# Gate and up projections of a two-layer decoder trunk: 18 of 22 blocks by Strassen's seven products

## The chip, the cores and the metric

One core of one Trainium2 chip runs the whole program. The metric is the device time of one execution in microseconds (us), lower is better. The kernel before took 1387.57 us, the median of three runs (1387.44 to 1389.32).

## What is computed

Two layers, each a token mixer (a gated linear recurrence and sparse attention side by side, not touched here) and a feed-forward block, each followed by a layer norm of `ALPHA * x + sublayer(x)`. All tensors are float32: x has 512 tokens of 1024 values, the hidden width D_FF is 2816.

```python
def layer_norm(x, g, b, eps=1e-5):
    mu = jnp.mean(x, -1, keepdims=True)
    var = jnp.mean(jnp.square(x - mu), -1, keepdims=True)
    return (x - mu) * lax.rsqrt(var + eps) * g + b

for l in range(DEPTH):                                   # DEPTH = 2
    mix = token_mixer(x, l) @ w_out[l]
    x = layer_norm(ALPHA * x + mix, ln1_g[l], ln1_b[l])
    ffn = (jax.nn.silu(x @ w_ffn_gate[l]) * (x @ w_ffn_up[l])) @ w_ffn_down[l]
    x = layer_norm(ALPHA * x + ffn, ln2_g[l], ln2_b[l])
```

The change concerns `x @ w_ffn_gate` and `x @ w_ffn_up`, and what comes right behind them.

## The kernel before

**Precision.** Float32 operands go to TensorE as two parts, a rounded high part and the remainder (type fp32r). `mm3` (lines 77 to 82) makes one product of three matmuls: high x high (L79), high x low (L80), low x high (L81). In the trace, xh and xl are the parts of x, whi and wlo those of a weight.

**Weights.** `load_w` (L53 to L75) loads 512 KB of raw weight by SP's DMA queue into one of two buffers (wraw, L57), casts it on ScalarE to the high part (L73) and subtracts on VectorE for the low part (L74). There are three buffers each for whi and wlo. A helper tag `"a"` splits into one of eleven large buffers instead, where the weight can be kept.

**Gate and up.** The 2816 hidden columns are 22 blocks of 128. For each block there is one product for gate and one for up: `feat_mm` runs 8 steps over the 1024 inputs, each with `mm3` on all 512 tokens, so 24 matmuls of 512 columns. The weight stands still in the array, the tokens stream, and the result is 128 hidden columns x 512 tokens in a PSUM bank (tag "d", two banks). `feats` runs the blocks one after the other; only the first five products (`LEAD2`) go by halves of 256 tokens, since x arrives by halves from `norm_turn` (the norm ahead of the stage, which turns the rows by TensorE transposes and splits them). `ffn` takes each result: Silu on ScalarE for gate (L845), and for up the product on VectorE (L851) and the split of the hidden block into its two parts (L852, L853), which stay in SBUF.

**Down.** `wide_mm` takes hidden blocks as the stationary operand and streams 512 columns of the down weight. The first pass does the left 512 output columns of all four token tiles; then come tiles 0 and 1, and tiles 2 and 3, for the right ones. The last three weights of one pass are kept for the next. In the last layer four more weights (`held`, tag "a") are kept for the very end, where tile 2 runs its last matmuls ahead of tile 3, so that the output norm of tile 2 (`norm`, L617 on) lies beside the matmuls of tile 3.

**The order.** A scheduler (the Tile framework) orders the instructions of each engine by its own simulation and by priorities; `tc.high_priority(offset=...)` moves an instruction ahead. SP's queue carries the weight loads. POOL (GpSimd) issues the DMAs of its own queue (bias strips, residual rows, norm parameters) and computes the powers of the norms (L354, L614). The buffers of the mixer (bias strips and the like) are used again by tag when they are free. The lines that carry most of the stage:

```python
def feat_mm(self, pt, w, x, n0=0, n1=S, k0=0, k1=NK):                       # L85
    for k in range(k0, k1):
        self.mm3(pt[:, n0:n1], *w(k * 128, 128), XH[k // 4][:, k % 4, n0:n1],
                 XL[k // 4][:, k % 4, n0:n1], k == 0, k == NK - 1)
srcs = [s for u in range(NF) for s in (io["wg"][l, u], io["wu"][l, u])]
self.feats(srcs[:5], x1, ffn, LEAD2)
self.norm_rest(l, 0, rows, None)
self.feats(srcs[5:], x1, lambda i, pt: ffn(i + 5, pt))
held = (0, 1, 2, 3) if last else (0,)
late = list(held) if last else []
```

## Time and profile before

| | |
|---|---|
| median of three runs | 1387.57 us (1387.44 to 1389.32) |
| the profiled execution, its own time | 1386.79 us |
| its span in the profile | 1385.0 us |
| TensorE (PE) busy | 97% of the span |
| VectorE (DVE) busy | 54% |
| ScalarE (ACT) busy | 43% |
| GpSimd (POOL) busy | 8% |
| mean granted TensorE clock | 0.996 of full speed |

The profile is of one execution; its time is the span and 1.8 us around it. PE rows are matmuls, PEld rows are the loads of the stationary operand, which run beside them. Matmuls overlap one another, so the duration of one row is longer than the distance from its start to the next one's: the distance is what the stream costs.

### The profile page before, as it was taken

Reading aid. Unit: us, or ns where it says so; the run is one execution under the profiler, and the core shown is the slowest. Engines: PE = TensorE matmul, PEld = TensorE weight load, DVE = VectorE, ACT = ScalarE, POOL = GpSimd, SP = SyncE. Lnnn points to the kernel's source line nnn. Section 1 sums busy time; section 2 is a strip of 40 time slices with the busy share of each in tenths; the row PEclk is TensorE's granted clock in tenths of the full one; section 3 lists DMA queues with packets and bytes.
Section 4 is the critical chain, followed back from the end, with each engine's and each line's share of the span. In section 5 each row is a group of like instructions: output and inputs, shape, how many; then the busy total and the mean of one; then the engine's idle time right before and its main releaser. Section 6 shows DMA issues by size and latency. Waiting matters only on the chain.

```text
span 1385.0 us, 19299 instructions
## 1 busy us (share of the span) xinstructions
PE 1349.5 (97%) x7548; PEld 1172.0 (85%) x7548; DVE 754.4 (54%) x1483; ACT 594.1 (43%) x1109; POOL 106.8 (8%) x179
## 2 busy tenths in 40 slices
PE   7999999999999999999999999999999999999997
PEld 6978999789888888888889889987998888888885
DVE  4755898865633333224468568988636333332344
ACT  4244777844332232222443558777353232232220
POOL 2230111100000000000112001110000000000001
PEclk9999999999999999999999999999999999999999
DMA  6253213132222322234543222120413322322332
GB/s 225 87 148 113 77 56 105 42 118 88 73 96 91 106 91 94 104 104 140 182 135 113 77 84 77 61 100 32 137 47 122 106 92 93 106 91 96 132 107 92
DMA packets 39371, 139.84 MB, mean 101 GB/s; under 512 B 5188, under 2 KB 5348, under 8 KB 38768
## 3 DMA queue, kind: packets, MB, share of 16 engines
q1 hardware_dynamic: 31392, 112.93, 24.1%
q0 software_dynamic: 6736, 23.58, 5.3%
q10 hardware_dynamic: 1152, 2.10, 0.5%
q8 instruction: 59, 0.97, 0.3%
q14 instruction: 32, 0.26, 0.1%
HBM read 134.34 MB, written 7.10 MB: 102 GB/s over the span
## 4 chain that ended last, share of the span: by engine, by line
PE 88%; DMA 4%; ACT 3%; DVE 2%; issue 1%; POOL 0%; POOLq 0%; DVEq 0%; SPq 0%; ACTq 0%
PE ps_d L79 20%; PE ps_d L80 20%; PE ps_d L81 19%; PE ps_s L81 3%; PE ps_s L80 3%; PE ps_s L79 3%; PE ps_t L547 2%; PE ps_t L80 1%; PE ps_t L81 1%; PE ps_t L79 1%; PE ps_h L292 1%; PE ps_o L558 1%; PE ps_o L81 1%; PE ps_o L80 1%; PE ps_o L79 1%
## 5 line engine op out<-in xcount | busy, mean ns | idle before, releaser
L73 ACT CAST whi<-wraw 128x1024 fp32r<-128x1024 f32 (+1 forms) x190 | 199.3, 1049 | 534.3 <-PE ps_d L80 201.6
L74 DVE TENSOR_TENSOR wlo<-wraw,whi 128x1024 fp32r<-128x1024 f32 (+1 forms) x190 | 232.2, 1222 | 305.8 <-ACT whi L73 300.5
L79 PE MATMUL ps_d<-xh,whi 128*128 128x512 f32 (+1 forms) x888 | 338.2, 382 | 1.9 <-ACT gates L398 1.8
L81 PE MATMUL ps_d<-xh,wlo 128*128 128x512 f32 (+1 forms) x888 | 338.4, 381 | 0.0
L80 PE MATMUL ps_d<-xl,whi 128*128 128x512 f32 (+1 forms) x888 | 338.3, 381 | 0.0
L79 PEld LDWEIGHTS ps_d<-xh,whi 128*128 128x128 f32 x888 | 166.9, 188 | 33.0 <-ACT gates L398 1.9
L80 PEld LDWEIGHTS ps_d<-xl,whi 128*128 128x128 f32 x888 | 167.2, 188 | 31.9 <-issue 0.7
L81 PEld LDWEIGHTS ps_d<-xh,wlo 128*128 128x128 f32 x888 | 167.1, 188 | 31.2
L851 DVE TENSOR_TENSOR silu<-ps_d,silu 128x512 f32<-128x512 f32 x42 | 29.0, 691 | 130.0 <-PE ps_d L81 128.6
L79 PE MATMUL ps_d<-whi,xh 128*128 128x256 f32 (+1 forms) x304 | 90.8, 300 | 0.0
L80 PE MATMUL ps_d<-wlo,xh 128*128 128x256 f32 (+1 forms) x304 | 89.1, 294 | 0.0
L81 PE MATMUL ps_d<-whi,xl 128*128 128x256 f32 (+1 forms) x304 | 88.2, 291 | 0.0
L508 ACT ACTIVATE e<-e,mn 128x128 f32<-128x128 f32 (+3 forms) x128 | 71.6, 561 | 13.8 <-DVE mn L506 13.1
L614 POOL TENSOR_TENSOR rstd<-mv,mhalf 128x1 f32<-128x1 f32 x16 | 17.7, 1109 | 735.2 <-DVE mv L612 735.2
L506 DVE CUSTOM_DVE_ANT_0 e<-ps_s,strip 128x128 f32<-128x128 f32 (+3 forms) x128 | 59.2, 484 | 6.8 <-PE ps_s L521 5.9
L80 PEld LDWEIGHTS ps_d<-wlo,xh 128*128 128x128 f32 x304 | 58.3, 192 | 2.1 <-issue 1.4
L552 DVE TENSOR_TENSOR ptl<-ps_t,pth 128x384 fp32r<-128x384 f32 (+1 forms) x96 | 56.8, 595 | 5.5 <-ACT pth L551 4.7
L79 PEld LDWEIGHTS ps_d<-whi,xh 128*128 128x128 f32 x304 | 58.1, 192 | 1.8 <-issue 0.7
L551 ACT CAST pth<-ps_t 128x384 fp32r<-128x384 f32 (+1 forms) x96 | 48.7, 510 | 24.9 <-PE ps_t L547 17.4
L81 PEld LDWEIGHTS ps_d<-whi,xl 128*128 128x128 f32 x304 | 58.1, 191 | 0.7
L547 PE MATMUL ps_t<-ident,e 128*128 128x128 f32 x320 | 53.4, 273 | 0.3 <-ACT e L532 0.2
L324 DVE TENSOR_TENSOR hgKQ<-hgKQ,hgF 128x512 f32<-128x512 f32 x64 | 43.7, 686 | 6.0 <-PE ps_h L292 2.9
(475 smaller groups left out, 2590.0 us busy)
## 6 DMA issues: line engine op xcount, KB each, us to landing
wraw<-in_wd SPq DMA_DIRECT2D x55, 512.0 KB, 3.3
wraw<-in_wg SPq DMA_DIRECT2D x44, 512.0 KB, 3.2
wraw<-in_wu SPq DMA_DIRECT2D x44, 512.0 KB, 3.3
wraw<-in_wf SPq DMA_DIRECT2D x32, 512.0 KB, 3.6
wraw<-in_wt SPq DMA_DIRECT2D x16, 512.0 KB, 3.5
wraw<-in_wo SPq DMA_DIRECT2D x16, 512.0 KB, 3.2
w<-in_w POOLq DMA_DIRECT2D x16, 256.0 KB, 5.0
strip<-Z POOLq DMA_DIRECT2D x16, 256.0 KB, 3.0
```

The lines of the kernel that those rows point to most:

```text
L73: nc.scalar.copy(h, raw[:, i:i + n])
L74: nc.vector.tensor_tensor(o, raw[:, i:i + n], h.bitcast(F32), op=OP.subtract)
L79: first = t.matmul(out, ah, bh, start=start, stop=False)
L80: t.matmul(out, ah, bl, start=False, stop=False)
L81: t.matmul(out, al, bh, start=False, stop=stop)
L324: nc.vector.tensor_tensor(both, both, f, op=OP.mult)
L506: nc.vector.tensor_tensor_reduce(out=e, in0=pa, in1=st[:, 512 - pa.shape[-1]:], scale=1.0, scalar=3e38, op0=OP.add, op1=OP.min, accum_out=mn)
L508: nc.scalar.activation(e, e, AF.Exp, bias=mn, scale=-1.0, accum_out=sm)
L547: nc.tensor.transpose(p[:, c:c + 128], E[qt][:, j * 128:(j + 1) * 128], self.ident)
L551: nc.scalar.copy(ph[:, :c], p[:, :c])
L552: nc.vector.tensor_tensor(pl[:, :c], p[:, :c], ph[:, :c].bitcast(F32), op=OP.subtract)
L851: nc.vector.tensor_tensor(s, pt, s, op=OP.mult)
```

## The change

18 of the 22 blocks (4 to 21) of gate and of up are taken two by two. For such a pair, a unit, the weight is a matrix of 2 x 2 quarters (two blocks of 128 hidden columns x two halves of 512 inputs), and x one of 2 x 2 quarters (two halves of inputs, `R1.` and `R2.`, x two halves of 256 tokens, `R.1` and `R.2`). The four quarters of the result come from seven products of quarters (Strassen's scheme in Winograd's form) where eight are needed otherwise. A product has 4 steps x 3 matmuls of 256 columns, 12 matmuls. There are 9 pairs x 2 weights x 2 layers = 36 units.

- **Sums of x** (T1 to T4) are formed and split once per layer on VectorE and ScalarE, from the raw x1 that `norm_turn` now writes into buffers that stay.
- **Sums of weights**, four per unit. s1 and s3 come from a plain load on SP's queue and a second DMA on POOL's queue that adds to what is there (`accum_op`). The other two are formed on VectorE in the buffer of the raw weight.
- **Splits.** Each of the seven left operands is split on its own, 512 columns at a time (L111 on ScalarE, L112 on VectorE), into a ring of six places that is cut from the three whi and wlo buffers.
- **Sums of products.** A, D and B are accumulators of 256 columns in banks "d", "t", "s". Four products go into A and two into D, with a copy (sx, sy, su) taken by ScalarE in between; VectorE adds the copies to get the quarters. The last two products of a unit are placed among the next unit's.
- **Hidden blocks.** Blocks 0 to 5 are split at once; the other 16 stay whole in float32 and are split beside the first down pass into the large buffers, four at first and then two per step.
- **The end of the last layer.** The large buffers are taken, so nothing is held from the pass of tiles 0 and 1; the four late weights (now blocks 4 to 7 of the down weight's steps) are loaded again.

```diff
+    def stage(self, sa, sb):
+        with self.tc.high_priority(offset=3000):
+            a = self.sb.tile([128, 1024], F32, name="wraw", tag="wr", bufs=2)
+            s1, s3, d = (self.sb.tile([128, 512], F32, name=n, tag=t, bufs=2) for n, t in (("ws1", "st"), ("ws3", "pc"), ("wd", "wd")))
+            nc.sync.dma_start(s1, sb[:, 512:])
+            nc.sync.dma_start(s3, sa[:, :512])
+            nc.gpsimd.dma_start(s1, sb[:, :512], accum_op=OP.add)
+            nc.gpsimd.dma_start(s3, sb[:, :512], accum_op=OP.add)
+            nc.sync.dma_start(a, sa)
+            nc.sync.dma_start(d, sb[:, 512:])
+        return a, s1, s3, d
+
+    def split(self, raw):
+        h, o = self.ring[self.place % 6]
+        self.place += 1
+        with self.tc.high_priority(offset=3000):
+            nc.scalar.copy(h, raw)
+            nc.vector.tensor_tensor(o, raw, h.bitcast(F32), op=OP.subtract)
+        return h, o
+
+    def prod(self, acc, raw, R, start):
+        L = self.split(raw)
+        for k in range(4):
+            self.mm3(acc, *(p[:, k * 128:(k + 1) * 128] for p in L), *(p[:, k] for p in R), start and k == 0, k == 3,
+                     skip_group_check=not start)
+
+    def seven(self, units, R):
...
+        for unit in units + [None]:
+            if unit:
+                a, s1, s3, d = self.stage(*unit[:2])
+                A, B, D = (self.ps(t)[:, :256] for t in "dst")
+                self.prod(A, a[:, :512], R["R11"], True)
+                x = copy("sx", A)
+            if old:
+                old[0]()
+            if unit:
+                self.prod(D, s1, R["T1"], True)
+                y = copy("sy", D)
+                with self.tc.high_priority(offset=3000):
+                    nc.vector.tensor_tensor(a[:, :512], s1, a[:, :512], op=OP.add)
+                self.prod(B, a[:, 512:], R["R21"], True)
+                unit[2]("11", B, x)
+            if old:
+                old[1]()
+            if unit:
+                self.prod(A, a[:, :512], R["T2"], False)
+                u = copy("su", A)
+                with self.tc.high_priority(offset=3000):
+                    nc.vector.tensor_tensor(a[:, 512:], a[:, :512], a[:, 512:], op=OP.add)
+                self.prod(D, a[:, 512:], R["R22"], False)
+                unit[2]("12", D, u)
+                def third(A=A, s3=s3, y=y, take=unit[2]):
+                    self.prod(A, s3, R["T3"], False)
+                    take("22", A, y)
+                def fourth(A=A, d=d, take=unit[2]):
+                    self.prod(A, d, R["T4"], False)
+                    take("21", A, None)
+                old = (third, fourth)
...
-        srcs = [s for u in range(NF) for s in (io["wg"][l, u], io["wu"][l, u])]
+        srcs = [io[w][l, j] for j in range(4) for w in ("wg", "wu")]
...
+        self.seven([(io[w][l, j], io[w][l, j + 1], f(j)) for j in range(4, NF, 2) for w, f in (("wg", gate), ("wu", up))], R)
...
-        held = (0, 1, 2, 3) if last else (0,)
+        held = () if last else (0,)
...
-        late = list(held) if last else []
+        late = (4, 5, 6, 7) if last else ()
...
+        for i in late:
+            kept[i] = down_w(1, i, "a")
```

The takers `gate` and `up` (new lines 989 to 1014) add a copy to an accumulator's quarter on VectorE where the scheme wants it (L1009 for up), and then apply Silu on ScalarE (gate) or the product of gate and up on VectorE (up, L1011).

**VectorE, in the middle of gate and up of layer 0, before.** wlo is the split of a weight, silu the product of up and gate, h_f a split of a hidden block; per block (two weights) there are four instructions.

```order
L74 TENSOR_TENSOR wlo_4519<-wraw_4516,whi_4518 128x1024
L853 TENSOR_TENSOR h_f_3613<-silu_4413,h_f_3613 128x512
L74 TENSOR_TENSOR wlo_4552<-wraw_4549,whi_4551 128x1024
L851 TENSOR_TENSOR silu_4480<-ps_d_4488,silu_4480 128x512
L74 TENSOR_TENSOR wlo_4586<-wraw_4583,whi_4585 128x1024
```

**The same place of the change.** Here ws1 and ws3 are the sums by DMA, wraw and wd raw weights, sx and su copies of accumulators, up_5494 the up quarters that are being added together.

```order
L112 TENSOR_TENSOR wlo_4047<-wraw_5544,whi_4046 128x512
L112 TENSOR_TENSOR wlo_4047<-ws3_5420,whi_4046 128x512
L147 TENSOR_TENSOR wraw_5544<-ws1_5545,wraw_5544 128x512
L1009 TENSOR_TENSOR up_5494<-ps_s_5429,sx_5445 128x256
L112 TENSOR_TENSOR wlo_4043<-ws1_5545,whi_4042 128x512
L112 TENSOR_TENSOR wlo_4043<-wraw_5544,whi_4042 128x512
L156 TENSOR_TENSOR wraw_5544<-wraw_5544 128x512
L112 TENSOR_TENSOR wlo_4045<-wd_5421,whi_4044 128x512
L1009 TENSOR_TENSOR up_5494<-ps_t_5430,su_5525 128x256
L112 TENSOR_TENSOR wlo_4045<-wraw_5544,whi_4044 128x512
L1011 TENSOR_TENSOR h_e_5367<-up_5494,h_e_5367 128x512
L112 TENSOR_TENSOR wlo_4043<-ws3_5546,whi_4042 128x512
```

Splits are now half as long and stand between sums of weights (L147, L156) and additions from PSUM (L1009); a gate and an up unit together have 27 instructions on VectorE, 25 of them between the split of one ws1 buffer and the addition L147 that reads the next contents of the same buffer. On PE, the products of two units alternate so that 24 to 28 matmuls stand between two additions to the same accumulator with a copy or an addition between them.

**SP's queue, at the end of layer 0's mixer, before:** the last two output weights (in_wo), then the first of gate and up.

```order
L57 DMA wraw_3256<-in_wo 128x1024
L57 DMA wraw_3262<-in_wo 128x1024
L57 DMA wraw_3637<-in_wg 128x1024
L57 DMA wraw_3644<-in_wu 128x1024
L57 DMA wraw_3651<-in_wg 128x1024
```

**The same place of the change:**

```order
L97 DMA ws1_4049<-in_wg 128x512
L97 DMA ws1_4145<-in_wu 128x512
L57 DMA wraw_3256<-in_wo 128x1024
L98 DMA ws3_4050<-in_wg 128x512
L98 DMA ws3_4146<-in_wu 128x512
L57 DMA wraw_3262<-in_wo 128x1024
L57 DMA wraw_3628<-in_wg 128x1024
```

The plain halves of the sums for the first two units are loaded ahead of the third and fourth output weight; their buffers are those of bias strips. On POOL, the two adding DMAs of ws1 stand between the four powers of the mixer's last part (L354 before, L440 now), the second of them right ahead of the last power.

**VectorE at the end of the program, before.** r are the rows of a token tile, ps_o and ps_h the accumulators of tiles 2 and 3 in the last pass.

```order
L874 SCALAR_TENSOR_TENSOR r<-r,ps_o 128x512
L875 BN_STATS st<-r 128x6
L611 BN_AGGR mv<-st 128x2
L612 TENSOR_SCALAR mv<-mv 128x1
L621 SCALAR_TENSOR_TENSOR r<-r,mv,lnp 128x1024
L624 SCALAR_TENSOR_TENSOR r<-r,rstd,lnp 128x1024
L874 SCALAR_TENSOR_TENSOR r<-r,ps_h 128x512
L875 BN_STATS st<-r 128x6
L611 BN_AGGR mv<-st 128x2
```

**The same place of the change:**

```order
L1050 SCALAR_TENSOR_TENSOR r<-r,ps_o 128x512
L1051 BN_STATS st<-r 128x6
L1050 SCALAR_TENSOR_TENSOR r<-r,ps_h 128x512
L697 BN_AGGR mv<-st 128x2
L1051 BN_STATS st<-r 128x6
L698 TENSOR_SCALAR mv<-mv 128x1
L707 SCALAR_TENSOR_TENSOR r<-r,mv,lnp 128x1024
L697 BN_AGGR mv<-st 128x2
L710 SCALAR_TENSOR_TENSOR r<-r,rstd,lnp 128x1024
```

The two tiles' chains now alternate: on PE the matmuls of tiles 2 and 3 are interleaved, and ps_o ends 5 matmuls ahead of ps_h, where it ended 24 ahead before.

## Rows read from the trace of the kernel before

**Rows 1.** The page, busy time of each engine and share of the span.

```profile
PE 1349.5 (97%) x7548; PEld 1172.0 (85%) x7548; DVE 754.4 (54%) x1483; ACT 594.1 (43%) x1109; POOL 106.8 (8%) x179
```

**Rows 2.** By stretch: length, busy (count) PE PEld DVE ACT POOL, clock, DMA share, GB/s.

```profile
329.00:358.00 29.00, 29.00 (x244) 28.84 (x245) 9.32 (x18) 16.87 (x27) 1.96 (x3) 1.00 0.21 74
358.00:564.60 206.60, 206.60 (x922) 171.42 (x921) 80.42 (x86) 59.52 (x76) 0.00 (x0) 1.00 0.28 95
564.60:625.00 60.40, 60.40 (x267) 49.86 (x266) 15.91 (x14) 13.57 (x14) 0.00 (x0) 1.00 0.31 105
```

**Rows 3.** PE's timeline (start, duration, instruction): 512-column matmuls, first and last of 13.

```profile
361.64 0.39 PE L80 MATMUL ps_d<-xl,whi 128*128 128x512 f32 x1
...
364.36 0.39 PE L80 MATMUL ps_d<-xl,whi 128*128 128x512 f32 x1
```

**Rows 4.** PE's timeline in the lead blocks: 256-column matmuls, first and last of 17.

```profile
340.73 0.28 PE L81 MATMUL ps_d<-xh,wlo 128*128 128x256 f32 x1
...
342.64 0.28 PE L81 MATMUL ps_s<-xh,wx 128*128 128x256 f32 x1
```

**Rows 5.** Groups, 329 to 343 us, weight loads: count, busy, mean ns, idle before.

```profile
L81 PEld LDWEIGHTS ps_s<-xh,wx 128*128 128x128 f32 x14 | 2.6, 188 | 0.0
```

**Rows 6.** Groups by form, whole span, VectorE.

```profile
L74 DVE TENSOR_TENSOR wlo<-wraw,whi 128x1024 fp32r<-128x1024 f32 x186 | 228.1, 1226 | 300.0 <-ACT whi L73 294.7
...
L74 DVE TENSOR_TENSOR wx<-wraw,wx 128x512 fp32r<-128x512 f32 x24 | 16.3, 687 | 4.8 <-ACT wx L73 3.8 <-PE ps_o L566 0.9
...
L397 DVE TENSOR_TENSOR vt<-ps_d,vt 128x256 fp32r<-128x256 f32 x8 | 3.2, 417 | 0.0
```

**Rows 7.** Groups by form, whole span, ScalarE.

```profile
L845 ACT ACTIVATE silu<-ps_d 128x512 f32<-128x512 f32 x40 | 23.4, 585 | 0.0
...
L73 ACT CAST wx<-wraw 128x512 fp32r<-128x512 f32 x24 | 14.1, 618 | 18.1 <-DMA wraw<-in_wg 7.4 <-DMA wraw<-in_wu 3.7 <-DMA wraw<-in_wo 3.0
...
L295 ACT COPY atm<-ps_h 128x256 f32<-128x256 f32 x6 | 2.2, 365 | 9.5 <-PE ps_h L292 9.5
```

**Rows 8.** DMA issues: count, size of each, median us from issue to landing.

```profile
wraw<-in_wg SPq DMA_DIRECT2D x44, 512.0 KB, 3.2
...
strip<-Z POOLq DMA_DIRECT2D x16, 256.0 KB, 3.0
...
Z<-rv POOLq DMA_DIRECT2D x8, 320.0 KB, 9.8
```

**Rows 9.** DMA queues, POOL's: packets, MB, share of 16 engines.

```profile
q0 software_dynamic: 6736, 23.58, 5.3%
```

**Rows 10.** VectorE's timeline at the end, in brackets the idle time before.

```profile
1370.26 0.69 DVE L874 SCALAR_TENSOR_TENSOR r<-r,ps_o 128x512 f32<-128x512 f32 x1 [9.17 <-PE ps_o L81]
...
1373.73 1.28 DVE L624 SCALAR_TENSOR_TENSOR r<-r,rstd,lnp 128x1024 f32<-128x1024 f32 x1 [0.44 <-POOL rstd L614]
1375.70 0.69 DVE L874 SCALAR_TENSOR_TENSOR r<-r,ps_h 128x512 f32<-128x512 f32 x1 [0.68 <-PE ps_h L81]
...
1379.17 1.41 DVE L624 SCALAR_TENSOR_TENSOR r<-r,rstd,lnp 128x512 f32<-128x512 f32 x2 [0.44 <-POOL rstd L614]
```

**Rows 11.** PE's timeline: first and last L79 of the last pass, layers 0 and 1.

```profile
663.78 0.39 PE L79 MATMUL ps_o<-whi,h_qs 128*128 128x512 f32 x1
...
693.69 0.39 PE L79 MATMUL ps_h<-whi,h_qs 128*128 128x512 f32 x1
...
1346.86 0.39 PE L79 MATMUL ps_o<-whi,h_qs 128*128 128x512 f32 x1
...
1374.82 0.39 PE L79 MATMUL ps_h<-wa,hb 128*128 128x512 f32 x1
```

**Rows 12.** Timelines at the end of layer 0's mixer: VectorE, SP's queue, POOL.

```profile
273.98 0.69 DVE L506 CUSTOM_DVE_ANT_0 e<-ps_s,strip 128x512 f32<-128x512 f32 x1
...
277.90 0.33 SPq L57 DMA_DIRECT2D wraw<-in_wo  x1
...
279.00 1.04 POOL L354 TENSOR_TENSOR rs<-ss,mhalf 128x4 f32<-128x4 f32 x1 [3.43 <-DVE ss L352]
```

More of the change, by code (lines that the diff above doesn't have):

```diff
@@ new lines, in seven, with copy @@
+    def seven(self, units, R):
+        nc = self.nc
+        ts = [[self.sb.tile([128, 1024], F32R, name=n, tag=t, bufs=3) for n, t in (("whi", "wh"), ("wlo", "wl"))] for _ in range(3)]
+        self.ring = [[t[:, c:c + 512] for t in p] for p in ts for c in (0, 512)]
+        self.place = 0
+        def copy(name, src):
+            t = self.sb.tile([128, 256], F32, name=name, tag="a7", bufs=6)
+            with self.tc.high_priority(offset=4000):
+                nc.scalar.copy(t, src)
+            return t
+        old = None
+        for unit in units + [None]:
[29 more added lines that the diff above has]
+                old = (third, fourth)
@@ new lines, in gate, with take @@
+        def gate(j):
+            def take(part, acc, add):
+                if part == "11":
+                    raws[j], raws[j + 1] = hidden(j), hidden(j + 1)
+                g = raws[j + int(part[0]) - 1]
+                o = g[:, 256 * int(part[1]) - 256:256 * int(part[1])]
+                with tc.high_priority(offset=4000):
+                    if add is not None:
+                        nc.vector.tensor_tensor(o, acc, add, op=OP.add)
+                    if part == "12":
+                        nc.scalar.activation(g, g, AF.Silu)
+                    elif part[0] == "2":
+                        nc.scalar.activation(o, o if add is not None else acc, AF.Silu, scale=-1.0)
+            return take
```

118 lines of the change are left out of this document (91 added, 27 removed).

## The prediction

> **What bounds the kernel now.** I read the page's busy shares first: TensorE (PE) works 97% of the span, VectorE 54%, ScalarE 43% [rows 1]. Then the table by stretch, for the stage that is rewritten: from 358 us to 564.6 us, gate and up of layer 0, PE is busy all the time, with VectorE at 80 of 206.6 us, ScalarE at 60 and the DMA engines at 28% [rows 2]. A busy PE can still be slow, so the third view is PE's timeline. The 512-column matmuls of this stage each last 0.39 us there, but start every 0.227 us: the two rows are the first and the last of 13, 2.72 us apart [rows 3]. They overlap, nothing else is between them, and the stage lasts as many spacings as it has matmuls. So only PE's spacing and its number of matmuls count here, and everything else is free until it makes PE wait.
>
> **The change, part by part.**
>
> *Fewer, shorter matmuls.* A unit (one weight, two blocks) was 2 blocks x 8 x 3 = 48 matmuls of 512 columns, 48 x 0.2267 = 10.88 us. It is now 7 products x 4 x 3 = 84 of 256 columns. What one of these costs when the weights stand still and x streams can be read in the lead blocks of the same stage, which go by halves of the tokens: 17 rows, first and last 1.91 us apart, 16 spacings of 0.1194 us [rows 4]. So 84 x 0.1194 = 10.03 us. There are 9 pairs x 2 weights x 2 layers = 36 units: 36 x 0.85 = **-30.6 us**. The loss by half columns is thus small: two such matmuls take 0.239 us against 0.227 us. What speaks against it is the weight load, which is now twice as frequent for the same columns. Its rows read 0.188 us each in the same stretch [rows 5], longer than the 0.1194 us between matmuls, so successive loads must overlap one another or the matmuls. If they did not, they alone would take 84 x 0.188 = 15.8 us a unit, 36 x 4.9 = 177 us more than before; rows 4 exclude that for this very form. The Trainium skill (TensorE: Matmul & The Clock Gate, The mechanism) says that a weight load overlaps matmuls in flight only where it goes to another row group; by it the full-height loads here would lie between the matmuls and the change would lose. The rows of this case disagree with it.
>
> *VectorE and ScalarE in a unit.* VectorE now does 7 splits and 2 sums of 512 (0.687 us each), 3 additions of 256 from PSUM (0.417) and, for up, one product of 512 and two of 256 [rows 6]: 7.4 us for gate, 9.0 us for up, 8.2 of 10.03 us on the mean. ScalarE does 7 casts of 512 (0.618) and 3 copies of 256 from PSUM (0.365), and for gate a Silu of 512 and two of 256 (0.585 bounds the one, 0.365 the others) [rows 7]: 5.4 to 6.7 us. Neither reaches PE. What may cost is not the sum but a late hand-over: before PE may add to an accumulator again, a copy or an addition must have read it, and the order leaves 24 to 28 matmuls, 2.9 us or more, in between. Two splits already at work (1.4 us) and the addition itself (0.4) fit. No row shows such a chain at this load; I bound it by nothing and by 0.28 us a unit (one split's tail in every third unit or so), **0 to +10 us, taken +3**, since the spare ring places let the splits run several products ahead.
>
> *Loads.* A unit fetches 1792 KB where it fetched 1024: 183 GB/s over 10.03 us. Packets of the POOL queue moved 23.58 MB in 5.3% of 16 engines' span [rows 9], 321 GB/s when all work, so 5.7 us of each 10.03, or 7.3 if an adding DMA moves its bytes twice. The cover is the double buffers. The tile of s1 is free again after its split in one unit and its successor is wanted 25 VectorE instructions later, of 27 in two units: 18 us. In these lie the plain load (a load of twice its size lands in 3.2 us) and the adding DMA. Of the latter no row exists: its near end is the plain 256 KB transfer on POOL's queue, 3.0 us, its far end the slowest of that queue, 9.8 us for 320 KB [rows 8]. Even 3.2 + 9.8 fits into 18, so I cost it **nothing**; the nearer row in size and kind is the 3.0.  The raw weights have some 9 us for 3.2. The other cost would be throughput; that is a rival below.
>
> *The four sums of x.* 4 sums and 4 splits of 1024 on VectorE, at 1.23 us [rows 6] 9.8 us, and 4 casts on ScalarE, about 1 us each. They lie beside the lead blocks, where VectorE works 9.3 of 29 us [rows 2], and three plain blocks: **0**, and if that cover were gone, the first unit would wait some microseconds, twice.
>
> *Staged loads ahead of others.* The first two units' s1 tiles reuse the bias strips' buffers, so their loads stand on SP's queue ahead of the third output weight, and their adding DMAs stand on POOL's queue ahead of the last head's power. The last strip is read until 274.67 us; the output weight was issued at 277.90, the power at 279.00 [rows 12]. A load issued at 274.7 lands at about 277.9: **0**, with 1.1 us to spare; late, it would delay the end of the mixer by as much as it is late.
>
> *Splits of the hidden blocks.* 16 blocks x 2 halves are split beside the first down pass: 32 x 0.417 = 13.3 us of VectorE in 60 us, which has 15.9 busy [rows 2]. **0.**
>
> *The end.* The four weights of the last pass are no longer kept but loaded again, and the order now lets both last token tiles end together. The third tile's chain, 1370.26 to 1375.01, lay under the fourth's 24 matmuls; now only 5 matmuls (1.1 us) cover it [rows 10]. Of its 4.75 us, 0.44 were a wait that now gets filled, 1.1 stay covered: up to +3.2; with the fourth's own wait filled too, +1.9. **Taken +2.5.** The pass with these loads has its model in layer 0, where it loaded seven: from the first to the last of its rows 29.91 us, against 27.96 us in layer 1 with four kept [rows 11]. Next-layer loads disturb that one too: **0 to +2, taken +1.**
>
> *Elsewhere* the scheduler moves a few instructions (the first loads, the next layer's strips); 2 us either way, taken 0.
>
> **Sum.** The profiled execution took 1386.79 us (a span of 1385.0). 1386.8 - 30.6 + 3 + 2.5 + 1 = 1362.7. The median of the runs is 0.8 us above the profiled one: **1363.5 us**. The forecast's own bounds: all unknowns at their best 1355, all at their worst 1373.
>
> **The rivals.**
>
> *Late hand-overs eat a good part.* VectorE at 82% and in fixed order: if each of some 13 instructions a unit lost 0.1 us to the semaphore before it, an up unit would be 9.0 + 1.5 = 10.5 us, longer than its products, and waits at accumulators would come on top. At 0.3 to 0.6 us a unit beyond the forecast, 11 to 22 us: 1374 to 1385. For it: the chain sum, cast, subtraction, product is longer than the two steps before. Against it: the ring has six places. 14%.
>
> *Nothing changes.* The hand-overs take 0.85 us a unit, and 1385 to 1390 comes out. 3%.
>
> *The adding DMAs are the bound: slower.* They are two a unit. If they do not overlap one another, the stage goes at their pace once two take longer than the old 10.88 us, that is, from 5.4 us each. At 6.5 us each, 13 us a unit, 36 x 2.1 = +76 us: 1463 us; at the far end of 9.8 us each, +314 us. For it: no row shows what an addition on the way costs, and the row of 9.8 us is on the same queue. Against it: the plain rows of 3.0 us, mostly latency, since 256 KB take only 0.8 us of 16 engines by the rate above, and different DMAs can be under way together. 12%.
>
> *The weight load paces the stream*: 1387 + 177 = 1564 us. Rows 4 and 5 speak against it for this form. 1%.
>
> **How the numbers follow.** The forecast has 70%. Its point is the sum; 1355 to 1383 takes in the forecast's bounds and nearly all of the late hand-overs, and leaves out slower (13%), no change (3%) and a little at either end. A measurement of this kernel can tell about 0.2%, 2.8 us, from no change. Faster by more than that: 70 + 14 = 84%; within: 3%; slower: 13%.
>
> **What would show it.** Right: gate and up from the first unit to the last in 18 x 10.03 = 181 us a layer (195.8 before), 256-column matmuls 0.119 to 0.120 us apart, PE's waits there a few us in all, adding DMAs that land in 3 to 6 us, VectorE at about 80% of the stage, and a last chain on VectorE of some 7 to 8 us after the last matmul where it was 4.9. Wrong: PE rows with waits for VectorE or ScalarE in every unit (the first rival), VectorE's sums waiting for a DMA and POOL's queue full (the third), or a spacing near 0.19 us (the fourth).

## The result, and the profile after

The change takes **1363.88 us** (median of four runs, 1363.12 to 1365.61) where the kernel before took 1387.86 us beside it (1387.44 to 1389.32). The ratio is **0.9827, 95% interval 0.981 to 0.9844**: 24 us faster. The forecast was 1363.5. That it is met this closely is partly luck: two of its terms were wrong by about 3 us each, in opposite directions, and smaller errors cancelled as well. The profiled execution, 1363.12 us with a span of 1361.1, shows it.

Of the page, the busy shares and the two large DMA queues (packets, MB, share of 16 engines), which answer to [rows 1, 9]:

```profile
PE 1319.5 (97%) x8844; PEld 1209.3 (89%) x8844; DVE 937.9 (69%) x1913; ACT 719.5 (53%) x1459; POOL 169.7 (12%) x251
...
q1 hardware_dynamic: 42336, 124.47, 28.4%
q0 software_dynamic: 17104, 42.46, 13.6%
```

PE has more matmuls, and 30.0 us less to do. The table by stretch, with the columns of [rows 2]: first the lead and the plain blocks of layer 0, then its units.

```profile
328.00:373.00 45.00, 44.19 (x320) 41.49 (x319) 30.13 (x38) 26.14 (x40) 2.25 (x3) 1.00 0.17 60
373.00:552.00 179.00, 179.00 (x1477) 178.26 (x1476) 139.18 (x252) 102.84 (x215) 28.69 (x34) 1.00 0.69 174
```

In the units PE never stops. VectorE is at 78% (82% forecast), the DMA engines at 69% where they were at 28%. PE's timeline shows a unit: the first matmul of product B in a unit, and the matmul 84 places behind it.

```profile
379.82 0.28 PE L79 MATMUL ps_s<-xh,whi 128*128 128x256 f32 x1
...
389.90 0.28 PE L79 MATMUL ps_d<-th,whi 128*128 128x256 f32 x1
```

10.08 us, which is 84 x 0.1200. That is the mean over the stage too: nothing at all is lost between products.

To see where the 24 us came from, the span is cut at six matmuls which both kernels have: the first transpose of layer 0's first norm, the first matmul of its second down pass (tiles 0 and 1), its last down matmul, and the same three in layer 1. PE's timeline, before:

```profile
323.13 0.27 PE L642 MATMUL ps_t<-ident,r 128*128 128x128 f32 x1
632.26 0.39 PE L79 MATMUL ps_d<-wa,hb 128*128 128x512 f32 x1
694.14 0.39 PE L81 MATMUL ps_h<-whi,h_qs 128*128 128x512 f32 x1
1006.21 0.27 PE L642 MATMUL ps_t<-ident,r 128*128 128x128 f32 x1
1315.35 0.39 PE L79 MATMUL ps_d<-wa,hb 128*128 128x512 f32 x1
1375.27 0.39 PE L81 MATMUL ps_h<-wa,hb 128*128 128x512 f32 x1
```

And in the changed kernel:

```profile
322.96 0.27 PE L729 MATMUL ps_t<-ident,r 128*128 128x128 f32 x1
618.27 0.39 PE L79 MATMUL ps_d<-wa,h_at 128*128 128x512 f32 x1
679.88 0.39 PE L81 MATMUL ps_h<-whi,hb 128*128 128x512 f32 x1
995.46 0.27 PE L729 MATMUL ps_t<-ident,r 128*128 128x128 f32 x1
1289.77 0.39 PE L79 MATMUL ps_d<-whi,h_at 128*128 128x512 f32 x1
1349.39 0.39 PE L81 MATMUL ps_h<-wa,hb 128*128 128x512 f32 x1
```

The differences of these starts, and the spans of 1385.01 and 1361.06 us, give:

| stretch | before | change | difference | forecast |
|---|---|---|---|---|
| start to the norm of layer 0 | 323.13 | 322.96 | -0.17 | 0 |
| gate, up and first down pass, layer 0 | 309.13 | 295.31 | -13.82 | -13.8 |
| the other down passes, layer 0 | 61.88 | 61.61 | -0.27 | 0 |
| join and mixer of layer 1 | 312.07 | 315.58 | **+3.51** | 0 |
| gate, up and first down pass, layer 1 | 309.14 | 294.31 | -14.83 | -13.8 |
| the other down passes, layer 1 | 59.92 | 59.62 | -0.30 | +1 |
| behind the last matmul's start | 9.74 | 11.67 | +1.93 | +2.5 |
| sum | 1385.01 | 1361.06 | -23.95 | -24.1 |

So the two stretches with the units gave 28.65 us, and 4.70 net were lost again elsewhere. Three places lose, the first of them inside the units' stretch.

**Ahead of the first unit, layer 0: 1.0 us** (295.31 against 294.31 in layer 1, where it does not happen). VectorE's timeline, then PE's, with the idle time ahead in brackets:

```profile
364.05 4.63 DVE L741 TENSOR_TENSOR r<-r,lnp 128x1024 f32<-128x1024 f32 x4 [2.63 <-DMA lnp<-in_ln]
368.60 2.35 DVE L742 TENSOR_TENSOR r<-r,lnp 128x1024 f32<-128x1024 f32 x2
370.87 0.69 DVE L960 TENSOR_TENSOR silu<-ps_d,silu 128x512 f32<-128x512 f32 x1
...
371.61 0.50 PE L79 MATMUL ps_d<-xh,whi 128*128 128x512 f32 x1 [0.72 <-DVE silu L960]
```

The row work of the first norm (L741, L742) starts late, when its parameters (lnp) have landed. The product of gate and up (L960) stands behind six of its instructions, and PE wants the bank which that product reads. The parameters take one of the large buffers, which the raw x of the sums holds now: their load is issued at 356.51, behind the last split of these sums (L936), where the kernel before issued it at 331.92. It also lands late. The DMA view of this one load, in the change and in the run sums_dve further down, which has no adding DMA (KB, us to landing):

```profile
lnp<-in_ln POOLq DMA_DIRECT2D x1, 1024.0 KB, 7.5
...
lnp<-in_ln POOLq DMA_DIRECT2D x1, 1024.0 KB, 4.8
```

In sums_dve and best_dve, the two runs without adding DMAs, this 1.0 us is gone (294.30 and 294.29).

**At the join of the two layers: about 3 us.** PE waits there for the weights of the next mixer (sums in us, times, longest), and the stretches (length, PE busy, granted clock, DMA share, GB/s) show what goes with the waits:

```profile
PE ps_s L81 <- DVE wlo L74: 1.5, 1, 1.5
PE ps_o L79 <- ACT wx L73: 0.7, 1, 0.7
```

```profile
684.00:689.00 5.00, 5.00 (x44) 1.00 0.61 213
690.60:692.00 1.40, 0.00 (x0) 0.94 0.02 6
692.00:694.00 2.00, 1.96 (x9) 0.50 0.92 322
...
696.40:699.00 2.60, 2.60 (x24) 1.00 0.77 306
```

Before, PE waited once there, 1.1 us, and the granted clock stayed at full speed. Now, after two waits with two matmuls between them, it is 0.50 in the next stretch, 1.2 GHz for 2.4: 256-column matmuls start 0.214 us apart (692.63 to 694.98, eleven spacings) where 0.120 is usual. The fifteen spacings from 692.04 to 695.35 thus take 3.31 us for 1.80.

During the longer wait the DMA engines are nearly idle (0.02). What PE waits for then is a split on VectorE (L74). Its cast on ScalarE (L73) ended 2.9 us earlier, and row work stands between (L741, L742):

```profile
686.80 1.05 ACT L73 CAST whi<-wraw 128x1024 fp32r<-128x1024 f32 x1 [2.54 <-DVE r L1050]
...
690.77 1.22 DVE L74 TENSOR_TENSOR wlo<-wraw,whi 128x1024 fp32r<-128x1024 f32 x1
```

The kernel before has the same order on VectorE there, and its wait of 1.1 us.

**At the end: 1.93 us.** VectorE's timeline, which answers to [rows 10]:

```profile
1348.68 0.69 DVE L1050 SCALAR_TENSOR_TENSOR r<-r,ps_o 128x512 f32<-128x512 f32 x1 [2.49 <-PE ps_o L81]
...
1350.01 0.67 DVE L1050 SCALAR_TENSOR_TENSOR r<-r,ps_h 128x512 f32<-128x512 f32 x1
...
1353.09 1.28 DVE L710 SCALAR_TENSOR_TENSOR r<-r,rstd,lnp 128x1024 f32<-128x1024 f32 x1 [0.32 <-POOL rstd L700]
...
1356.07 1.41 DVE L710 SCALAR_TENSOR_TENSOR r<-r,rstd,lnp 128x512 f32<-128x512 f32 x2 [0.44 <-POOL rstd L700]
```

The two tiles' chains alternate on VectorE, 8.80 us from the first addition to the end, and the second tile's last matmuls cover only the start of it. From the start of the last matmul to VectorE's end it is 8.1 us where it was 5.3: 2.8 more. Both chains still wait for POOL (0.32 and 0.44 us). What comes behind VectorE is 0.8 us shorter, since the last store lands sooner (DMA view, before and then the change):

```profile
out_dram<-r SPq DMA_DIRECT2D x1, 256.0 KB, 3.1
...
out_dram<-r SPq DMA_DIRECT2D x1, 256.0 KB, 2.0
```

In the units the adding DMAs are hidden. Of the DMA view of the units of layer 0 (373 to 552 us), two queues and the two issues of adding DMAs (count, KB each, median us to landing):

```profile
q1 hardware_dynamic: 9564, 22.01, 39.0%
q0 software_dynamic: 4752, 8.88, 29.3%
...
ws<-in_wg POOLq DMA_DIRECT2D x16, 256.0 KB, 5.0
...
ws<-in_wu POOLq DMA_DIRECT2D x16, 256.0 KB, 4.5
```

They land in 4.5 to 5.0 us. But they are dear for the DMA engines: 8.88 MB in 29.3% of 179 us is 169 GB/s when all work, against 315 GB/s for the plain loads (22.01 MB in 39.0%), 1.86 times as long per byte. The size of the packets is not the reason: those of 2048 B took 195 ns each in the adding DMAs and 105 ns in the plain loads of this stretch. The Trainium skill (DMA: Bandwidth & Descriptors, Rules for kernel authors) says that an accumulating DMA reads its destination and writes it later. Such an additional read is in keeping with the factor; that it is the reason is not shown by any run here.

### The profile page after: what moved, and what is told of

It is laid out like the page before. It is cut to its first block, busy times and chain, and to the rows that moved or that the text cites. A ratio compares the mean times of both kernels' runs of the same rounds, so it can differ in the third digit from the quotient of the medians.

```text
span 1361.1 us, 23186 instructions
## 1 busy us (share of the span) xinstructions
PE 1319.5 (97%) x8844; PEld 1209.3 (89%) x8844; DVE 937.9 (69%) x1913; ACT 719.5 (53%) x1459; POOL 169.7 (12%) x251
## 4 chain that ended last, share of the span: by engine, by line
PE 86%; DMA 5%; DVE 3%; issue 3%; ACT 2%; POOL 1%; POOLq 0%; ACTq 0%; DVEq 0%; SPq 0%
PE ps_d L79 15%; PE ps_d L80 15%; PE ps_d L81 15%; PE ps_t L81 4%; PE ps_t L80 4%; PE ps_t L79 4%; PE ps_s L81 4%; PE ps_s L80 4%; PE ps_s L79 4%; PE ps_t L633 2%; PE ps_h L378 1%; DMA wraw<-in_wo 1%; PE ps_o L644 1%; PE ps_o L643 1%; PE ps_s L505 1%
## 5 line engine op out<-in xcount | busy, mean ns | idle before, releaser
L74 DVE TENSOR_TENSOR wlo<-wraw,whi 128x1024 fp32r<-128x1024 f32 (+1 forms) x122 | 149.0, 1222 | 164.0 <-ACT whi L73 163.9
L73 ACT CAST whi<-wraw 128x1024 fp32r<-128x1024 f32 (+1 forms) x122 | 127.7, 1048 | 237.4 <-PE ps_t L81 71.1
L79 PE MATMUL ps_d<-xh,whi 128*128 128x512 f32 (+1 forms) x456 | 154.1, 342 | 2.6 <-ACT gates L484 1.8
L81 PE MATMUL ps_d<-xh,wlo 128*128 128x512 f32 (+1 forms) x456 | 154.8, 340 | 0.0
L80 PE MATMUL ps_d<-xl,whi 128*128 128x512 f32 (+1 forms) x456 | 154.5, 340 | 0.0
L111 ACT CAST whi<-wraw 128x512 fp32r<-128x512 f32 x144 | 89.2, 622 | 123.4 <-PE ps_d L80 92.5
L112 DVE TENSOR_TENSOR wlo<-wraw,whi 128x512 fp32r<-128x512 f32 x144 | 98.4, 689 | 43.6 <-ACT whi L111 40.8
L80 PE MATMUL ps_d<-tl,whi 128*128 128x256 f32 x432 | 121.5, 283 | 0.0
L81 PE MATMUL ps_d<-th,wlo 128*128 128x256 f32 x432 | 120.5, 283 | 0.0
L79 PE MATMUL ps_d<-th,whi 128*128 128x256 f32 x432 | 120.3, 283 | 0.0
L79 PEld LDWEIGHTS ps_d<-xh,whi 128*128 128x128 f32 x456 | 85.9, 190 | 11.5 <-ACT gates L484 2.0
L79 PE MATMUL ps_d<-whi,xh 128*128 128x256 f32 (+1 forms) x304 | 90.2, 298 | 0.0
L80 PEld LDWEIGHTS ps_d<-tl,whi 128*128 128x128 f32 x432 | 82.9, 192 | 0.2
L79 PEld LDWEIGHTS ps_d<-th,whi 128*128 128x128 f32 x432 | 82.2, 192 | 0.2
```

Source lines behind the costliest of these rows:

```text
L73: nc.scalar.copy(h, raw[:, i:i + n])
L74: nc.vector.tensor_tensor(o, raw[:, i:i + n], h.bitcast(F32), op=OP.subtract)
L79: first = t.matmul(out, ah, bh, start=start, stop=False, **kw)
L80: t.matmul(out, ah, bl, start=False, stop=False, **kw)
L81: t.matmul(out, al, bh, start=False, stop=stop, **kw)
L111: nc.scalar.copy(h, raw)
```

## The experiments

The theory going in: PE's number of matmuls times their spacing gives the gain; the hand-overs and the adding DMAs cost nothing; what is lost is lost by the new places of the hidden blocks and late weights. Twelve runs, in the same cuts, in us (gate, up and first down pass of layer 0; its other down passes; gate, up and first down pass of layer 1; the join with layer 1's mixer; all behind the first down pass of layer 1). Where several executions were timed, the ratio is to runs of before on the same chip.

| run | gate/up, 0 | passes, 0 | gate/up, 1 | join, mixer | end | median us | ratio |
|---|---|---|---|---|---|---|---|
| before | 309.13 | 61.88 | 309.14 | 312.07 | 69.66 | | |
| the change | 295.31 | 61.61 | 294.31 | 315.58 | 71.29 | 1363.88 | 0.9827 |
| eight | 320.67 | 61.88 | 320.67 | 311.54 | 69.52 | 1406.59 | one run |
| layout | 308.92 | 63.11 | 308.93 | 313.51 | 70.83 | 1391.28 | 1.0045 (1.0028 to 1.0062) |
| add2 | 308.34 | 61.56 | 310.81 | 321.15 | 71.30 | 1397.98 | one run |
| add3 | 379.88 | 62.28 | 377.26 | 325.33 | 71.63 | 1548.88 | one run |
| sums_dve | 294.30 | 62.90 | 294.29 | 315.07 | 71.04 | 1362.72 | 0.9824 (0.981 to 0.9839) |
| ring3 | 296.28 | 61.77 | 295.14 | 315.86 | 71.28 | 1364.31 | one run |
| ring2 | 302.49 | 61.53 | 303.01 | 315.10 | 71.28 | 1380.43 | one run |
| join | 295.17 | 61.58 | 294.31 | 312.76 | 71.27 | 1361.42 | 0.9815 (0.9801 to 0.983) |
| rest | 295.49 | 61.57 | 295.91 | 316.19 | 71.48 | 1367.59 | 0.9856 (0.9839 to 0.9872) |
| tail | 295.16 | 61.63 | 294.31 | 316.65 | 71.23 | 1364.2 | 0.9835 (0.9812 to 0.9859) |
| best | 295.29 | 61.58 | 294.31 | 311.94 | 70.91 | 1363.28 | 0.9839 (0.9823 to 0.9856) |
| best_dve | 294.29 | 61.58 | 294.30 | 312.72 | 70.55 | 1358.03 | 0.9792 (0.9775 to 0.9809) |

The start, up to layer 0's norm, is left out of the table: it took between 320.1 and 330.7 us in these profiles, with nearly the same work in it (the first units' staged loads lie there). Part of its spread goes with the clock. In the change, ring3, best and best_dve the granted clock is 1.00 from 16 us to the norm, and the start takes 320.1 to 323.0 us. In before, eight, layout, sums_dve, ring2, join, rest and tail it is 0.50 for 3.4 to 6.8 us between 93 and 102 us, and the start takes 320.5 to 325.8. Whole times thus vary by more than the cuts behind the start do. These agree to some tenths where nothing was changed, the other passes of layer 0 and the join with its mixer only to 1.3 us (62.90 in sums_dve, 316.65 in tail). Each profile is of one execution: that of best took 1358.17 us, that of tail 1366.82.

**What half columns cost.** In the kernel before, each of the 18 blocks by two halves of the tokens, without Strassen:

```diff
-                self.feat_mm(pt, w, x)
+                if len(srcs) == 39 and i >= 3:
+                    self.feat_mm(pt, w, x, 0, 256)
+                    self.feat_mm(pt, w, x, 256, 512)
+                else:
+                    self.feat_mm(pt, w, x)
```

> The kernel before, with each of the last 18 blocks' products taken as two halves of 256 tokens: eight products of quarters a unit, no Strassen, nothing else changed. Theory (only the number of matmuls and their spacing count): a unit becomes 96 matmuls of 256 columns at 0.120 us, 11.52 us for 10.88, so 36 x 0.64 = +23 us on the 1387.6 before: 1408 to 1412. Rival (half columns cost nothing, and the seven products lost their gain elsewhere): 1388. Rival (the weight load sets the pace of short matmuls): 96 x 0.188 = 18 us a unit, 1645.

Measured: 320.67 - 309.13 = +11.54 us a layer, 36 x 0.641. The stage's row of the table by stretch:

```profile
400.00:560.00 160.00, 160.00 (x1335) 160.00 (x1334) 51.29 (x55) 43.62 (x56) 0.00 (x0) 1.00 0.30 93
```

PE is full and the granted clock whole; 1500 matmuls from 380 to 560 us are 0.1200 apart. So half columns cost 0.64 us a unit (11.52 us for eight products where 10.88 were needed), and the product that Strassen's scheme leaves out gives 1.44: 0.80 net. Neither rival's number came. The whole time, one execution, is 1406.59 us, just under the 1408 to 1412 expected; before took 1385.63 on this chip.

**The change without its units.**

```diff
-        self.seven([...], R)
+        self.feats([io[w][l, j] for j in range(4, NF) for w in ("wg", "wu")], x1, plain)
```

(`plain` is Silu, then the product, into the whole hidden blocks; the sums of x go too.)

> The change without the units: the 18 blocks plain, one after the other as before, no sums of x and of weights; but the hidden blocks whole and split beside the down pass, and the end of the last layer as in the change. Theory (the units alone give the gain; what the trace of the change lost at the join of the layers, +3.0, in the second mixer, +0.6, and behind the last matmul, +1.9, comes from the new places of the hidden blocks and of the late weights): before +4 to +6, 1391 to 1394, the join and the tail as in the change. Rival (the loss at the join comes from the units' loads or the sums of x): join as before, 1389 to 1390.

Measured: gate and up as before (-0.2 us), and the losses are there without any unit: the down passes of layer 0, the join and the mixer take 376.62 us (63.11 + 313.51), before 373.95, in the change 377.19. The end is 1.17 us longer than before, in the change 1.63. The timed ratio says +3.9 to +8.6 us, the profile's cuts +3.4. So most of what was lost belongs to the layout, not to Strassen; where in the join it falls differs (it starts in the last pass here, with +1.2).

**The margin of the adding DMAs.** Each twice, and three times, in a row. These two kernels add a quarter of the weights twice or three times to the sums, so they no longer compute the projections and serve for the time alone. The edit for two:

```diff
             nc.gpsimd.dma_start(s1, sb[:, :512], accum_op=OP.add)
+            nc.gpsimd.dma_start(s1, sb[:, :512], accum_op=OP.add)
             nc.gpsimd.dma_start(s3, sb[:, :512], accum_op=OP.add)
+            nc.gpsimd.dma_start(s3, sb[:, :512], accum_op=OP.add)
```

> The change with each adding DMA issued twice in a row (a quarter of the weights is added twice to the sums). Theory of latency, the prediction's: load 3.1 + 2 x 4.8 us = 12.7 us fits into the 18 us between a buffer's split and the next use: 1362 to 1367. Rival of throughput: in the change's stage the adding packets took 29% and the others 39% of 16 engines' time, so this one asks for 39 + 2 x 29 = 98%: loads land late, 1367 to 1380.

> The change with each adding DMA issued three times in a row. Theory of latency: 3.1 + 3 x 4.8 = 17.5 us, just at the 18 us: 1364 to 1375. Rival of throughput: 39 + 3 x 29 = 127% of the 181 us of the units in a layer, 2 x 0.27 x 181 = +98 us: 1440 to 1470.

Measured: +13.0 and +16.5 us in the two layers' stages for two, +84.6 and +83.0 for three. Both theories of both runs fall, latency clearly. The throughput theory has the right sign but is too small: 1397.98 us where its range was 1367 to 1380, and 1548.88 where it was 1440 to 1470. The units of layer 0 with two, by stretch, their POOL queue of DMAs, and what POOL itself waited for:

```profile
373.00:565.00 192.00, 182.73 (x1472) 180.44 (x1471) 134.84 (x247) 100.73 (x214) 55.97 (x66) 0.98 0.90 205
```

```profile
q0 software_dynamic: 9360, 17.27, 53.2%
```

```profile
POOL ws L102 <- DMA ws<-in_wg: 40.8, 8, 7.8
POOL ws L102 <- DMA ws<-in_wu: 34.3, 8, 5.8
```

The DMA engines are at 90%, and the adding packets move 17.27 MB in 53.2% of 192 us, 169 GB/s again. On top of that POOL works its queue in order: a second addition to a buffer waits there for the first to land, and the DMAs of the next sum stand behind it. How the loss divides between the two was not tried apart. The repeated additions for a layer's first units also stand ahead of powers of the mixer on this queue. PE's wait for hy, which is made with a power, grows at the end of layer 0's mixer from 0.6 us in the change to 1.3 and 3.3, and the cut with join and mixer is 5.6 and 9.8 us longer. With three, the stage:

```profile
373.00:644.00 271.00, 217.41 (x1505) 209.66 (x1504) 142.85 (x256) 102.04 (x218) 84.01 (x98) 0.87 0.84 176
```

With PE's waits the mean granted clock is lower too, 0.87. So the forecast's rival of the adding DMAs was nearer than its price said: one more addition per sum, and the stage goes at their pace.

**No adding DMA at all.** All four sums on VectorE:

```diff
-            nc.sync.dma_start(s1, sb[:, 512:])
-            nc.sync.dma_start(s3, sa[:, :512])
-            nc.gpsimd.dma_start(s1, sb[:, :512], accum_op=OP.add)
-            nc.gpsimd.dma_start(s3, sb[:, :512], accum_op=OP.add)
+            nc.sync.dma_start(s1, sb[:, :512])
             nc.sync.dma_start(a, sa)
             nc.sync.dma_start(d, sb[:, 512:])
+            nc.vector.tensor_tensor(s3, a[:, :512], s1, op=OP.add)
+            nc.vector.tensor_tensor(s1, s1, d, op=OP.add)
```

> The change with all four sums of weights on VectorE and no adding DMA (1024 KB a unit for 1792). Theory of room: VectorE goes from 139 to 139 + 36 x 0.69 = 164 of the 181 us of a layer's units, DMA from 69% to about 33%; neither makes PE wait: within 3 us of the change. Rival of late hand-overs: an up unit has 9.0 + 1.4 = 10.4 us of VectorE work for 10.08 us of products; at 0.3 to 0.6 us a unit, 11 to 22 us slower than the change. Rival of contention: without the adding DMAs splits and loads get faster, 1 to 3 us faster than the change.

Measured: 0.9824 against 0.9827, no difference. The units of layer 0:

```profile
373.00:552.00 179.00, 179.00 (x1472) 178.03 (x1471) 156.12 (x283) 103.95 (x215) 1.07 (x2) 1.00 0.34 102
```

VectorE at 87%, DMA at 34%, and PE does not wait once. The theory of room holds, and the rival of late hand-overs does not come even with two more instructions a unit. The rival of contention is right in one place: layer 0's stage is 1.0 us shorter, the wait ahead of the first unit (the parameters land after 4.8 us for 7.5). The whole time does not show it; the passes of layer 0 are 1.3 us longer here. The two adding DMAs spare VectorE 17 us a layer that nobody needs.

**The ring.** Three and two places of the six:

```diff
-        h, o = self.ring[self.place % 6]
+        h, o = self.ring[self.place % 3]
```

> The change with three of the six places of the ring of splits in use. Theory of room: a split has two products (2.9 us) for a sum, a cast and a subtraction, 0.69 + 0.62 + 0.69 = 2.0 us: within 4 us of the change. Rival (the six places are what hides irregular hand-overs): 0.3 to 0.6 us a unit, 11 to 22 us slower than the change, with waits of PE for whi and wlo in most units.

> The change with two of the six places of the ring. Theory: a split can only begin when the product two places back has ended, so it has the 1.44 us of one product for a cast and a subtraction of 1.31 us, with the waits between three engines on top, and other work on VectorE in between: 0.2 to 0.6 us late per product, 7 x 36 = 252 products: 50 to 150 us slower than the change, 1414 to 1515. Rival (the scheduler's order already hides what is left): under 10 us.

Measured: three places cost 0.8 to 1.0 us a layer, two 7.2 and 8.7. So three are enough, and hand-overs begin to cost with two; but 16 us in all lie between the 50 to 150 that I expected of that run and the 10 of its rival. A product begins with a matmul of the high part, which can start while the low part is still being subtracted. The expectation did not count this; that it is the reason was not tried.

**The join.** The down weight of step 2 (hidden blocks 4 and 5) is kept in layer 0 and comes first in the last pass:

```diff
-        held = () if last else (0,)
+        held = () if last else (2,)
-        order = [*range(n - 3, n), *held, ...]
+        order = [*held, *range(n - 3, n), ...]
```

> The change, but layer 0 keeps the down weight of hidden blocks 4 and 5 (not that of 0 and 1) for the last pass and takes it first there, so that the buffers from which the next layer's w1 loads wait are free 13 us earlier. Theory (those 1 MB of w1 and the 1 MB of norm parameters behind them collide with the weight loads at the join): the stretch from the last matmul of layer 0 to the next transposes goes from 18.95 back to 15.5 to 17.0 us, 2 to 3.5 us faster than the change. Rival (row work on VectorE or the clock at half speed is the cause, whatever the loads do): it stays at 18 to 19.5.

Measured: the cut with join and mixer falls from 315.58 to 312.76 us, before 312.07, and PE no longer waits for weights there. (The transposes at which I had meant to measure come 7 us earlier, since the scheduler moved other work of the mixer behind them; join and mixer together are what counts.) The reason stands on POOL's queue. In the change, the four loads of w1 (w) and the parameters of the norm:

```profile
663.89 1.14 POOL L504 DMA_DIRECT2D w<-in_w  x2 [10.05 <-PE ps_h L81]
665.68 1.07 POOL L504 DMA_DIRECT2D w<-in_w  x2 [0.66 <-PE ps_h L81]
666.74 0.54 POOL L690 DMA_DIRECT2D lnp<-in_ln  x1
```

With the other order:

```profile
645.68 1.08 POOL L504 DMA_DIRECT2D w<-in_w  x2 [101.01 <-PE ps_h L81]
652.02 1.06 POOL L504 DMA_DIRECT2D w<-in_w  x2 [5.26 <-PE ps_h L81]
...
654.81 0.58 POOL L690 DMA_DIRECT2D lnp<-in_ln  x1
```

The loads of w1 wait until the matmuls into ps_h have used the hidden blocks in their buffers ("pt"). Those are blocks 4 and 5 now, the sixth step of the last pass; before they were the last two blocks, its third step, and the first load was issued 24.4 us ahead of the last matmul of the pass (669.73 us), now 16.0. In the change, 2 MB on POOL's queue meet the last two down weights, which land 4.8 and 6.7 us after their issue; with the other order they take 3.5 and 4.1.

That the order gives this gain holds beyond one profile. The passes of layer 0 and the join with its mixer take, together, 373.5 to 374.3 us in the three runs with this order (join, best, best_dve), 376.6 to 378.3 in the seven with the change's (add2 and add3 left aside), 373.4 and 374.0 in eight and before. How it gives it is shown less well, for the order of VectorE changed along. The split for which PE waited 1.5 us now runs right behind its cast, and the row work (L741, from 687.34) behind both:

```profile
684.75 1.05 ACT L73 CAST whi<-wraw 128x1024 fp32r<-128x1024 f32 x1 [1.44 <-DMA wraw<-in_wf]
...
686.15 1.21 DVE L74 TENSOR_TENSOR wlo<-wraw,whi 128x1024 fp32r<-128x1024 f32 x1
```

What the earlier loads and what the order on VectorE are worth by themselves was not tried, so the row work of the rival is not excluded. The clock is not the cause: in layout it stays at 1.00 here with the loss, and in best_dve it falls to 0.50 for 3.4 us (from 694.29) with the gain.

**The row work ahead of the first unit,** moved behind the first splits of hidden blocks:

```diff
-        self.norm_rest(l, 0, rows, None)
         self.feats(srcs[5:], ...)
...
+            if i == 0:
+                self.norm_rest(l, 0, rows, None, self.first)
```

> The change with the row work of the first norm (eight VectorE instructions of 1.2 us a layer) moved behind the first splits of hidden blocks in the down pass. Theory: the 0.9 us that PE waits in layer 0 ahead of the first unit, for a product behind this row work, goes; the down pass has the room: 0.5 to 1.5 us faster than the change. Rival (the row work now delays the splits of hidden blocks): PE waits in the down pass, 1 to 3 us slower.

Measured: the wait goes, but PE now waits for a split of a down weight (wlo, L74) in the down pass, which makes it 0.75 us late in layer 0 and 1.2 in layer 1, where the stage is 1.6 us longer. The rival is right, and my remedy is none.

**The end.** Two late weights in an order that is held:

```diff
-        late = (4, 5, 6, 7) if last else ()
+        late = (0, 1) if last else ()
...
+            self.behind = self.latest
```

(Every late matmul of tile 3 depends on the last one of tile 2.)

> The change with two late weights (those of hidden blocks 0 to 3) instead of four in the last layer, and an order that holds: all matmuls of tile 2 with them, 12, ahead of the 12 of tile 3. Theory (the tail of 11.7 us is two norm chains of 4.75 us that alternate on VectorE, since only 5 matmuls lie between the ends of the two tiles): cover 12 x 0.227 = 2.7 us for 1.1, tail 10.0 to 10.3; the last weight may come 0.7 us late on PE: 0.5 to 1.6 us faster than the change. Rival (the late weights arrive so late that the order is taken back by waits of PE): the wait in the last pass is as long as the tail gets shorter, within 0.4 us of the change.

Measured: the tail shrinks from 11.67 to 10.16 us, as expected, and the pass in front of it grows from 59.61 to 61.07; together -0.06 us. PE's timeline of that pass has the wait:

```profile
1350.81 0.50 PE L80 MATMUL ps_o<-wa,h_at 128*128 128x512 f32 x1 [0.54 <-DVE wa L74]
```

The start of this row is 0.70 us late; another 0.6 us lies in matmuls some hundredths apart more than usual earlier in the passes, for which I have no cause. The rival is right: what the tail gains, the pass in front of it loses, about half of it at a wait for the last weight's split.

**Together.** Join and end, and the same with all sums on VectorE:

> The change with the order of the down weights of the run with the join and the end of the run with the tail. Theory: both gains add up, 2.5 to 4.5 us faster than the change, 0.979 to 0.981 of before. Rival (one of them only moves a wait): 0.9815, as with the join alone.

> The same, and all four sums of weights on VectorE, no adding DMA. Theory (neither VectorE at 87% nor DMA at 69% bounds the units): within 1.5 us of the run with the adding DMAs. Rival (the collision at the join was also one with the adding DMAs of the next stage): 2 us faster or more.

Measured: best, 0.9839, does not differ from the change in its timed runs, which spread from 1358.17 to 1366.08, though its cuts are 4.1 us shorter than the change's behind the start. The expected 0.979 to 0.981 thus did not come. The mean granted clock of these executions falls as their time rises, from 0.998 at the fastest to 0.993 at the slowest. best_dve is 0.9792 (0.9775 to 0.9809), **1358.03 us** where before took 1386.38 beside it, the fastest version of the study. Its cuts are 0.6 us shorter than those of best, so the 5 us between their medians lie in the start or in the spread of the executions; the medians are on the side of the rival (2 us or more), the cuts on that of the theory. What sets the start's time was not tried, and that the adding DMAs cost 5 us is not shown. The cuts show 1.0 us, in layer 0's stage.

## Why the prediction was right, point by point

*Matmuls, -30.6.* Right in kind, off by 1.8: at 0.1200 us a unit takes 10.08 and not 10.03 us, 36 x 0.80 = 28.8. I had 16 spacings of rows that are given to 0.01 us [rows 4], which leaves 0.0006 us of error in each, and 3024 matmuls multiply it. The runs eight and change count 1500 spacings. The rule of the Trainium skill (TensorE: Matmul & The Clock Gate, The mechanism) was told too narrowly in the prediction, which took a line of it that names the row group alone: its text lets a weight load overlap matmuls where it goes to another row group *or to the background weight buffer*. The trace is in keeping with the second half, in every unit: full-height loads of 0.192 us lie beside matmuls 0.120 us apart.

*Late hand-overs, 0 to +10, taken +3.* Measured 0. This is one of the two terms that failed, inside its bounds. VectorE at 78% in fixed order keeps up because splits are made ahead of their products, and ring3 and sums_dve show that there is more room still. The rival that made this cost large (14%) is refuted by them.

*Loads and adding DMAs, nothing.* Right in the units: 4.5 to 5.0 us to landing, inside 3 to 6. A nearer row than the 3.0 stood on the page before: the plain 256 KB loads of w on POOL's queue (w<-in_w), 5.0 us. Not priced was what the adding DMAs do to another load, the parameters of layer 0's norm (7.5 us to landing for 4.8), which is part of the 1.0 us below. And the margin was mis-sized. I priced the latency, with 18 us of room; the runs add2 and add3 show that the resources are the DMA engines' time, 1.86 times that of a plain byte, and POOL's order.

*Sums of x, nothing; some microseconds if the cover goes.* 1.0 us once, in layer 0: the sums hold the buffer of the norm's parameters, whose load therefore goes out 24.6 us later than before and meets the adding DMAs. In layer 1, and without adding DMAs, the wait does not come.

*Staged loads, splits of the hidden blocks:* nothing, as forecast. PE's wait for hy at the end of layer 0's mixer is 0.6 us, as before, and gate, up and first down pass of layer 1 are 294.31 us, 0.4 better than 309.14 less 18 x 0.80.

*The end, +1.9 to +3.2, taken +2.5.* Measured +1.93, but not for the reason given for the lower end. The second tile's own wait for POOL is not filled (0.44 us, and 0.32 at the first tile's). VectorE's end lies 2.8 us later behind the last matmul, and 0.8 came back from a store that landed sooner, which no term had. The lower bound itself does not follow from the rows: 3.2 less a wait of 0.44 is 2.8, not 1.9.

*Last pass, 0 to +2, taken +1.* Measured -0.30, just outside these bounds.

*Elsewhere, 2 us either way, taken 0.* This is the other term that failed: +3.51 at the join and in layer 1's mixer, outside the 2 us allowed. I had looked at buffers that the units take from the mixer of the same layer, not at buffers that the hidden blocks give back to the next one. Layout shows that the loss comes without the units, join that the order of the last pass gives most of it back; whether by the loads alone or by the row work's place on VectorE too is open.

The two errors cancel: +3 for hand-overs that did not come, +3 at a place where I had put nothing. So do the smaller ones: 1.8 and 1.0 us too hopeful for the spacing and ahead of the first unit, 1.3 and 0.6 too gloomy for the last pass and the end. That the forecast was met within 0.4 us is luck; that the gain is the saved matmuls, less some microseconds, is not.

## What to carry to other kernels

Where one engine works all the time, the gain of an algorithm is its instructions' number times a spacing that a long run of the same form shows; count some hundred spacings for it, not sixteen. When a layout changes, follow each buffer to its next user, in the *next* stage above all, and see what its load will then collide with: the losses at the join and ahead of the first unit begin there. A resource at 70% that looks free by latency may not bear twice the work: price its throughput and its queue's order too.

## What was not expected of the hardware

- Two spacings of this study, 0.2267 us at 512 columns and 0.1200 at 256, differ by 0.1067 us; that is 256 columns at 2.4 GHz, and leaves 0.0133 us fixed in each matmul. The Trainium skill (TensorE: Matmul & The Clock Gate, Back-to-back issue gap) gives columns at 2.4 GHz plus about 2.5 ns for a matmul in isolation: the slope agrees, the fixed part of these fp32r matmuls is 13.3 ns. It is why halving the columns costs 0.64 us a unit. At the granted 0.50 of the join the spacing, 0.2136 us, is that of 256 columns at 1.2 GHz with nothing left over, so the fixed part shows at the full clock alone.
- An adding DMA moved 165 to 169 GB/s of 16 engines' time in the change, add2 and add3 alike, plain loads 315 in the change.
- Two waits of PE close together at the join, with two matmuls between them, and the granted clock fell to 0.50 in the stretch behind them; before, one wait of 1.1 us at this place left it at 1.00. But in layout two waits there of 1.2 and 0.9 us, as close together, left it at 1.00 too, so these waits alone do not tell when it falls.
